# Strassen weight differences in slots on another grid, and one product of 512 columns at the head of each Strassen tile

## The chip, the cores and the metric

The kernel runs on one core of one Trainium2 chip. The engines are TensorE (PE in the profile; its weight loads are PEld), VectorE (DVE), ScalarE (ACT), GpSimd (POOL) and SyncE (SP, which issues the DMAs). The metric is the device time of one execution in microseconds, as the median of several runs.

## What is computed

A trunk of two layers on x with 256 rows and a width of 2048, all in float32. Layer 0 is a recurrent block, layer 1 attention over a sliding window; each is followed by a SwiGLU FFN with 5632 hidden columns. The change touches the first half of the FFN:

```python
def swiglu_ffn(x, g, w_in, w_out):
    h = rms_norm(x, g)
    gate, up = jnp.split(h @ w_in, 2, axis=-1)
    return x + (jax.nn.silu(gate) * up) @ w_out
```

## The kernel before

**Products.** TensorE multiplies in a float32 format that keeps fewer bits, so every operand is split into a high part and a low part (`hi`, `lo`), and one product becomes three: high by high, high by low, low by high. A weight tile of 128 x 1024 arrives by DMA in `raw`; ScalarE copies it to `hi` (L306, L299) and VectorE subtracts to get `lo` (L309, L300). `raw`, `hi` and `lo` are rings of four tiles. The x tiles and everything else live in 58 slots of 128 x 512 (`s0` to `s57`), handed out by `slot` and given back by `free`; x keeps its high part in the first 256 columns of a slot and its low part in the others.

An ordinary job works one weight tile off: 48 products of 256 columns with weights from hi/lo and the moving operand from a slot (L375; in the profile `b<-s,hi` means output, moving operand, weights). A product can also be 512 columns wide: it takes the high and the low part of x in one go and writes two halves of a PSUM bank. `products` makes them in runs of three (`RUNS`) where a bank has both halves free; the jobs between Strassen tiles share banks and have none.

**Strassen tiles.** In each FFN the first four column groups (`NS`) are done with seven multiplications of half blocks in place of eight (Strassen's scheme in Winograd's form). Each group has eight tiles, `c` from 0 to 7, so an FFN has 32. A tile is 7 x 3 = 21 products of 256 columns (L476) into four banks, here with weights from slots (x tiles, and sums of x tiles made by `form`) and the moving operand from hi/lo (`b<-hi,s`) or from slots that hold differences of weight blocks (`b<-s,s`). Between two Strassen tiles stand two ordinary jobs (`OWN`). The differences: GpSimd makes them from `raw` (`sums`, L279 to L281), ScalarE copies the high parts (L289), VectorE subtracts for the low parts (L291). `split_sums` issues this two jobs ahead of the tile, behind the split of a weight tile on the same engines. Two sets of six slots alternate: s[0] and s[1] hold the differences, s[2] to s[5] the parts; before, s[4] holds the high and s[5] the low part of s[1], so a high part and its low part are in different slots. In the tiles 1 to 6 of a group the nine products with hi/lo come first, in the tiles 0 and 7 six of them come ahead of the first with a difference.

Behind the last tile of a group `fast` (L675 to L685) adds the four banks up to the outputs U and V on VectorE (L132); a task then does the gate with two activations and two operations of L136, transposes the result on TensorE (L386) and splits it.

**The planner.** Queues are filled in program order, but the tool that lowers the kernel may place an instruction later than it is written. Background tasks are run by `run_bg` twice a job: a credit per engine (`dve`, `act`) rises by the estimated time of all that is issued and falls by one tick each half job, not below -SPARE; a task's next step runs only while `dve` is below DVE_TICK and `act` below ACT_TICK. In FFN 1 tick and floor are 640 and 500 for VectorE; from the K/V projection on 740 and 1000 (`LATER`). An add of n columns books 69 + 1.042 n.

**Where tiles stand.** Tiles take addresses in the order of their first use. Behind the lo ring come `t`, `h`, two `rstd` tiles of 258 columns, and further tiles of 256 columns, then the slots.

Of the kernel before, what the change touches and what calls it, by code (L numbers as in the profile page):

```python
# [12 lines left out]
F32 = mybir.dt.float32  # L13
F32R = mybir.dt.float32r
AF = mybir.ActivationFunctionType
ALU = mybir.AluOpType

P = 128
# [31 lines left out]
class Trunk:  # L50
# [24 lines left out]
    def __init__(self, ctx, tc, dram):  # L75
        self.tc, self.nc, self.d = tc, tc.nc, dram
        nc = self.nc
        const = ctx.enter_context(tc.tile_pool(name="const", bufs=1))
        psum = ctx.enter_context(tc.tile_pool(name="psum", bufs=1, space=bass.MemoryType.PSUM))
        tmp = ctx.enter_context(tc.tile_pool(name="tmp", bufs=1))  # L80
        self.tmp = tmp
        self.par = const.tile([P, NPAR], F32, name="par")
        self.con = const.tile([P, NCON], F32, name="con")
        self.cc = const.tile([P, 32], F32, name="cc")
        self.x = [const.tile([P, 4, T], F32, name=f"x{i}") for i in range(4)]
        self.slots = deque(range(58))
        self.spool = const
        self.held = {}
        self.raw = [const.tile([P, 1024], F32, name=f"raw{i}") for i in range(4)]
        self.hi = [const.tile([P, 1024], F32R, name=f"hi{i}") for i in range(4)]  # L90
        self.lo = [const.tile([P, 1024], F32R, name=f"lo{i}") for i in range(4)]
        self.banks = deque(psum.tile([P, 512], F32, name=f"b{i}") for i in range(8))
        self.misc = 0
        self.started = False
        self.xin = 0
        self.other = None
        self.summing = False
        self.opening = None
        self.sets = None
        self.runs = 0  # L100
        self.since = 0
        self.hold = False
        self.tmps = deque(const.tile([P, T], F32, name=f"t{i}") for i in range(4))
        self.halves = deque(const.tile([P, T], F32, name=f"h{i}") for i in range(8))
        self.rstd = [const.tile([P, T + 2], F32, name=f"rstd{i}") for i in range(2)]
        self.acc = const.tile([P, T], F32, name="acc")
        self.sq = deque(const.tile([P, T], F32, name=f"sq{i}") for i in range(2))
        self.jobs = []
        self.bg = deque()
        self.tick = -2 * self.LD  # L110
        self.dve = 0.0
        self.act = 0.0
# [34 lines left out]
        self.nc.vector.reciprocal(out, a)  # L147


    def slot(self, dt=F32R):  # L150
        i = self.slots.popleft()
        s = self.spool.tile([P, 2 * T], dt, tag=f"s{i}", name=f"s{i}")
        self.held[id(s)] = (i, s)
        return s

    def free(self, s):
        self.slots.append(self.held.pop(id(s))[0])

    def half(self):
        if self.halves:  # L160
            return self.halves.popleft()
        s = self.slot(F32)
        h = s[:, 0:T]
        self.held[id(h)] = (s, h)
        return h
# [103 lines left out]
    def sums(self, i):  # L269

        raw, tt = self.raw[i % 4], self.nc.gpsimd.tensor_tensor
        if not self.sets:
            self.sets = deque([self.slot(F32), self.slot(F32)] + [self.slot() for _ in range(4)] for _ in range(2))
        s = self.sets.popleft()
        self.sets.append(s)
        self.jobs[i][2]["set"] = s
        b = raw[:, :].rearrange("p (b t) -> p b t", b=4)
        two = lambda q: q.rearrange("p (b t) -> p b t", b=2)
        tt(two(s[0][:, :]), b[:, 0:3:2, :], b[:, 1::-1, :], ALU.subtract)  # L279
        tt(s[1][:, 0:T], raw[:, 2 * T:3 * T], s[0][:, 0:T], ALU.subtract)  # L280
        tt(s[1][:, T:2 * T], raw[:, 3 * T:4 * T], s[1][:, 0:T], ALU.subtract)  # L281

    def split_sums(self, i):

        if len(self.jobs[i]) > 2:
            s = self.jobs[i][2]["set"]
            for z, a, b in ((s[0], s[2], s[3]), (s[1], s[4], s[5])):
                with self.tc.issue_after(self.behind[0]):
                    self.nc.scalar.activation(a, z, AF.Copy)  # L289
                with self.tc.issue_after(self.behind[1]):  # L290
                    self.nc.vector.tensor_tensor(b, z, a.bitcast(F32), ALU.subtract)  # L291
            self.dve += 1400
            self.act += 1200
# [152 lines left out]
    def strassen(self, src, xs, forms, done, last, left):  # L446

        st = {}
        jobs = []
        for c in range(ND // 2):  # L450
            part = {}

            def mm(hi, lo, c=c, part=part):
                if c == 0:
                    st["ps"] = [self.bank() for _ in range(4)]
                    st["begun"] = set()
                ps = st["ps"]
                x2 = [self.need(xs[2 * c + kt]) for kt in range(2)]
                fh, fl = self.need(forms[c])
                A = lambda kt, b: tuple(x2[kt][:, q + b * P:q + b * P + P] for q in (0, T))  # L460
                S = lambda n: tuple(q[:, n * P:n * P + P] for q in (fh, fl))
                B = lambda n: tuple(q[:, n * T:n * T + T] for q in (hi, lo))
                s = part["set"]
                t1, t3, t2, t4 = (tuple(s[n + q][:, h * T:h * T + T] for q in (0, 1)) for n in (2, 4) for h in range(2))
                todo = [(0, 0, A(0, 0), B(1)), (1, 1, A(1, 0), B(3)), (1, 0, S(1), t2), (2, 0, S(0), t1),
                        (2, 1, S(2), t3), (3, 0, S(3), B(2)), (3, 1, A(1, 1), t4)]
                if 0 < c < ND // 2 - 1:
                    todo = [todo[q] for q in (0, 1, 5, 3, 4, 2, 6)]
                if self.other is not None:
                    self.runs = self.RUNS  # L470
                    self.other = None
                for n, (b, h, w, m) in enumerate(todo):
                    if n == 4:
                        self.half_tick()
                    for i, j in ((0, 0), (0, 1), (1, 0)):
                        self.nc.tensor.matmul(ps[b][:, h * T:h * T + T], w[i], m[j], start=b not in st["begun"],  # L476
                                              stop=c == ND // 2 - 1 and i == 1, skip_group_check=True)
                        st["begun"].add(b)
                        self.since += 1
                left[0] -= 1  # L480
                if last and c == ND // 2 - 1:
                    for q in self.sets:
                        for t in q:
                            self.free(t)
                    self.sets = None
                if last:
                    for q in (fh, fl):
                        self.free(q)
                if c == ND // 2 - 1:
                    done(ps)  # L490
            jobs.append((src(c), mm, part))
        return jobs

# [63 lines left out]

    def prep_tile(self, k, gains):

        self.gained(k, gains)  # L560
        yield
        yield from self.squares(k)
# [91 lines left out]
    def ffn(self, l, xs, forms, r, gains, rn, out=None):  # L654
# [6 lines left out]
        def later(g, s):  # L661
            while left[0]:
                yield 1
            for h in range(2):
                while len(self.slots) < 2:
                    yield 1
                q = self.slot()
                self.split_act(q, s[:, h * T:h * T + T])
                hid[2 * g + h].ap = q
                hid[2 * g + h].ready = True  # L670
                yield
            self.free(s)

        for g in range(self.NS):
            def fast(ps, g=g):  # L675
                c1, U, V = self.t(), self.slot(F32), self.slot(F32)
                two = lambda q: q.rearrange("p (b t) -> p b t", b=2)
                twice = lambda q: q.unsqueeze(1).broadcast_to([P, 2, T])
                self.a(c1, ps[0][:, 0:T])
                self.tt(two(U[:, :]), two(ps[1][:, :]), twice(c1[:, :]), ALU.add)  # L680
                self.tt(two(V[:, :]), two(ps[2][:, :]), twice(U[:, 0:T]), ALU.add)
                self.tt(U[:, 0:T], ps[2][:, 0:T], V[:, T:2 * T], ALU.add)
                self.tt(V, ps[3], V, ALU.add)
                for b in ps:
                    self.free_bank(b)  # L685

                def task():
# [26 lines left out]
        for g in range(self.NS, NH // 2):  # L714
            def done(ps, g=g):
# [4 lines left out]
                def task():  # L720
# [3 lines left out]
                    for h in range(2):  # L724
# [3 lines left out]
                            self.tt(up, up, rs, ALU.mult)  # L728
                        self.a(ga, ga, AF.Silu)
                        yield  # L730
                        if both is not None or h == 0 and left[0]:
                            if h == 0:
                                both = self.slot(F32)
                            self.tt(both[:, h * T:h * T + T], ga, up, ALU.mult)
# [638 lines left out]
```

## Time and profile before

| | us |
|---|---|
| median of three runs (lowest, highest) | 1974.23 (1973.96, 1975.21) |
| the profiled execution | 1976.51 |
| its span, first to last instruction | 1974.7 |
| L476, products of Strassen tiles, 1344 | 8% of the chain |
| L375, ordinary products | 84% of the chain |

How to read it: the profile's chain is followed back from the last instruction to what released it each time, so its shares say which engine's work the time consists of. TensorE's matmuls overlap, and an engine that is "busy" the whole span can still work at a slower or a faster pace; the pace is the distance from one product's start to the next. A group's row has its count, the busy time of the group, the mean duration of one in ns, and the idle time of the engine ahead of them.

### The profile page before, as it was taken

The numbers are of one execution on the slowest core, as the hardware profiler recorded it, in microseconds if no ns is written. First come the engines' busy times: TensorE is split into PE (matmuls) and PEld (weight loads), VectorE is DVE, ScalarE is ACT, GpSimd is POOL, SyncE is SP. The second block draws the span as 40 slices with busy tenths as digits, with TensorE's granted clock in tenths as the row PEclk, the third lists the DMA queues.
The fourth block names the chain that finished last, engine by engine and source line by source line (L and its number), as shares of the span: only waits on it lengthen the run. The fifth ranks groups of instructions, "written<-read, shape, count | busy, mean of one in ns | idle before, by whom it ended". The sixth has DMA issues, their size and how long they took to land.

```text
span 1974.7 us, 40978 instructions
## 1 busy us (share of the span) xinstructions
PE 1966.7 (100%) x16762; PEld 1934.6 (98%) x16762; DVE 1428.8 (72%) x2073; ACT 1121.2 (57%) x1746; POOL 383.4 (19%) x356
## 2 busy tenths in 40 slices
PE   9999999999999999999999999999999999999999
PEld 9999999999999999999999889999999999999999
DVE  8988978988986655545668767888889665554443
ACT  6798766555555444434556776655556554444442
POOL 0000125555520000000002454354444000000000
PEclk9999999999999999999999999999999999999999
DMA  8555665665555555555555434565555656556664
GB/s 276 187 190 177 200 209 193 187 208 197 192 201 191 195 193 192 193 193 196 195 185 182 129 129 152 191 214 193 193 193 201 194 193 193 194 196 205 206 205 127
DMA packets 106204, 377.16 MB, mean 191 GB/s; under 512 B 11936, under 2 KB 14368, under 8 KB 106016
## 3 DMA queue, kind: packets, MB, share of 16 engines
q1 hardware_dynamic: 105408, 373.88, 57.7%
q8 instruction: 131, 2.15, 0.4%
q10 hardware_dynamic: 608, 0.66, 0.1%
q14 instruction: 57, 0.47, 0.1%
HBM read 371.88 MB, written 2.10 MB: 189 GB/s over the span
## 4 chain that ended last, share of the span: by engine, by line
PE 96%; DVE 2%; ACT 1%; issue 0%; POOL 0%; DMA 0%; ACTq 0%; DVEq 0%; POOLq 0%
PE b L375 84%; PE b L476 8%; PE b L386 1%; PE b L866 1%; PE b L383 1%; ACT s L123 1%; DVE lo L309 1%; PE b L1052 1%; ACT hi L306 0%; DVE s L1120 0%; DVE s L132 0%; DMA x<-in_x 0%; PE b L1061 0%; PE b L1062 0%; PE b L1063 0%
## 5 line engine op out<-in xcount | busy, mean ns | idle before, releaser
L375 PE MATMUL b<-s,hi 128*128 128x256 f32 (+1 forms) x9536 | 1301.0, 282 | 1.6 <-ACT s L123 1.0
L375 PEld LDWEIGHTS b<-s,hi 128*128 128x128 f32 x9536 | 1203.1, 188 | 21.4 <-ACT s L123 1.7
L309 DVE TENSOR_TENSOR lo<-raw,hi 128x1024 fp32r<-128x1024 f32 (+1 forms) x643 | 812.5, 1266 | 447.4 <-ACT hi L306 444.8
L306 ACT ACTIVATE hi<-raw 128x1024 fp32r<-128x1024 f32 (+1 forms) x643 | 676.0, 1054 | 588.6 <-PE b L375 508.1
L375 PE MATMUL b<-s,lo 128*128 128x256 f32 x4992 | 748.3, 277 | 0.0
L375 PEld LDWEIGHTS b<-s,lo 128*128 128x128 f32 x4992 | 651.0, 188 | 0.5
L279 POOL TENSOR_TENSOR s<-raw 128x512 f32<-128x512 f32 x64 | 120.8, 1888 | 233.3 <-DMA raw<-in_ffn_in 185.6
L291 DVE TENSOR_TENSOR s<-s,s 128x512 fp32r<-128x512 f32 x128 | 141.5, 1141 | 0.6 <-ACT s L289 0.3
L1142 POOL TENSOR_TENSOR s<-s 128x128 f32<-128x128 f32 x32 | 14.7, 462 | 537.0 <-ACT s L123 534.3
L476 PE MATMUL b<-s,s 128*128 128x256 f32 x768 | 105.6, 282 | 0.5 <-DVE s L291 0.5
L299 ACT ACTIVATE hi<-raw 128x768 fp32r<-128x768 f32 x64 | 54.1, 845 | 78.8 <-PE b L375 56.5
L476 PEld LDWEIGHTS b<-s,s 128*128 128x128 f32 x768 | 97.3, 189 | 0.8 <-DVE s L291 0.7
L123 ACT ACTIVATE s<-s 128x256 fp32r<-128x256 f32 (+3 forms) x180 | 69.1, 429 | 33.4 <-POOL s L508 19.5
L132 DVE TENSOR_TENSOR s<-s,s 128x256 fp32r<-128x256 f32 (+3 forms) x148 | 70.6, 509 | 19.8 <-ACT s L123 19.7
L476 PE MATMUL b<-hi,s 128*128 128x256 f32 x384 | 80.7, 281 | 0.0
L280 POOL TENSOR_TENSOR s<-raw,s 128x256 f32<-128x256 f32 x64 | 78.7, 1230 | 5.0
L300 DVE TENSOR_TENSOR lo<-raw,hi 128x768 fp32r<-128x768 f32 x64 | 70.5, 1102 | 12.6 <-PE b L375 8.1
L289 ACT ACTIVATE s<-s 128x512 fp32r<-128x512 f32 x128 | 73.6, 617 | 7.8 <-POOL s L281 7.8
L506 POOL TENSOR_TENSOR s<-s 128x128 f32<-128x128 f32 x16 | 14.0, 877 | 328.8 <-ACT s L123 328.8
L281 POOL TENSOR_TENSOR s<-raw,s 128x256 f32<-128x256 f32 x64 | 70.9, 1108 | 5.0
L476 PEld LDWEIGHTS b<-hi,s 128*128 128x128 f32 x384 | 64.6, 189 | 0.0
L123 ACT ACTIVATE s<-x,par 128x256 fp32r<-128x256 f32 (+1 forms) x112 | 52.6, 498 | 19.9 <-DVE x L132 13.5
(121 smaller groups left out, 1127.4 us busy)
## 6 DMA issues: line engine op xcount, KB each, us to landing
raw<-in_ffn_in SPq DMA_DIRECT2D x352, 512.0 KB, 3.5
raw<-in_ffn_out SPq DMA_DIRECT2D x176, 512.0 KB, 3.4
raw<-in_lru_in SPq DMA_DIRECT2D x62, 512.0 KB, 3.6
raw<-in_lru_out SPq DMA_DIRECT2D x32, 512.0 KB, 3.8
raw<-in_w_q SPq DMA_DIRECT2D x32, 512.0 KB, 3.4
raw<-in_w_o SPq DMA_DIRECT2D x32, 512.0 KB, 3.3
raw<-in_gate SPq DMA_DIRECT2D x8, 512.0 KB, 3.7
raw<-in_kv SPq DMA_DIRECT2D x8, 512.0 KB, 3.4
```

The source lines that it names most:

```text
L123: self.nc.scalar.activation(out, in_, func, **kw)
L132: self.nc.vector.tensor_tensor(out, a, b, op)
L279: tt(two(s[0][:, :]), b[:, 0:3:2, :], b[:, 1::-1, :], ALU.subtract)
L280: tt(s[1][:, 0:T], raw[:, 2 * T:3 * T], s[0][:, 0:T], ALU.subtract)
L281: tt(s[1][:, T:2 * T], raw[:, 3 * T:4 * T], s[1][:, 0:T], ALU.subtract)
L289: self.nc.scalar.activation(a, z, AF.Copy)
L291: self.nc.vector.tensor_tensor(b, z, a.bitcast(F32), ALU.subtract)
L300: low = self.nc.vector.tensor_tensor(lo[:, q], raw[:, q], hi[:, q].bitcast(F32), ALU.subtract)
L306: high = self.ins(self.nc.scalar.activation(hi[:, q], raw[:, q], AF.Copy))
L309: low = self.nc.vector.tensor_tensor(lo[:, q], raw[:, q], hi[:, q].bitcast(F32), ALU.subtract)
L375: self.nc.tensor.matmul(*args, **kw)
L476: self.nc.tensor.matmul(ps[b][:, h * T:h * T + T], w[i], m[j], start=b not in st["begun"], stop=c == ND // 2 - 1 and i == 1, skip_group_ch ...
```

## The change

The 58 slots become 50 ordinary ones and eight others (`odd`, slots 50 to 57), which are claimed right behind the lo ring. The four split slots of both difference sets are taken from these; outside the FFN's Strassen phase, float32 slots are taken from them where one is free. Conditions on free slots now count the 50 alone. s[1] is split in two halves: s[4] holds the high and low part of its first half, s[5] those of its second. So s[5] can be read by one product of 512 columns. Each tile begins with it: A(1,1) high by both parts of t4, into both halves of bank 0, followed by A(1,1) low by t4 high. A(0,0) by B(1) goes to bank 3 in its place, and `fast` is rewritten for it: one more copy on ScalarE, and three adds of 256 columns in place of one of 512. The order of the seven multiplications is new.

```diff
-        self.slots = deque(range(58))
+        self.slots = deque(range(50))
+        self.odd = deque(range(50, 58))
...
+        for i in self.odd:
+            self.spool.tile([P, 2 * T], F32R, tag=f"s{i}", name=f"s{i}")
...
-    def slot(self, dt=F32R):
-        i = self.slots.popleft()
+    def slot(self, dt=F32R, odd=None):
+        odd = bool(self.odd) and dt == F32 if odd is None else odd
+        i = (self.odd if odd else self.slots).popleft()
...
-            self.sets = deque([self.slot(F32), self.slot(F32)] + [self.slot() for _ in range(4)] for _ in range(2))
+            self.sets = deque([self.slot(F32, False) for _ in range(2)] + [self.slot(F32R, True) for _ in range(4)]
+                              for _ in range(2))
...
-            for z, a, b in ((s[0], s[2], s[3]), (s[1], s[4], s[5])):
+            for z, a, b in ((s[0], s[2], s[3]), (s[1][:, 0:T], s[4][:, 0:T], s[4][:, T:2 * T]),
+                            (s[1][:, T:2 * T], s[5][:, 0:T], s[5][:, T:2 * T])):
...
-                todo = [(0, 0, A(0, 0), B(1)), (1, 1, A(1, 0), B(3)), (1, 0, S(1), t2), (2, 0, S(0), t1),
-                        (2, 1, S(2), t3), (3, 0, S(3), B(2)), (3, 1, A(1, 1), t4)]
+                todo = [(0, 0, A(1, 1), t4), (3, 1, A(0, 0), B(1)), (1, 0, S(1), t2), (1, 1, A(1, 0), B(3)),
+                        (2, 0, S(0), t1), (2, 1, S(2), t3), (3, 0, S(3), B(2))]
                 if 0 < c < ND // 2 - 1:
-                    todo = [todo[q] for q in (0, 1, 5, 3, 4, 2, 6)]
+                    todo = [todo[q] for q in (0, 1, 3, 6, 4, 5, 2)]
...
-                    for i, j in ((0, 0), (0, 1), (1, 0)):
+                    if n == 0:
+                        self.nc.tensor.matmul(ps[b], w[0], s[5], start=b not in st["begun"],
+                                              stop=c == ND // 2 - 1, skip_group_check=True)
+                        st["begun"].add(b)
+                    for i, j in ((0, 0), (0, 1), (1, 0))[2 * (n == 0):]:
...
     def prep_tile(self, k, gains):
+        while len(self.slots) < 3:
+            yield 1
...
-                while len(self.slots) < 2:
+                while len(self.slots) < 4:
...
-                c1, U, V = self.t(), self.slot(F32), self.slot(F32)
+                c1, c4, U, V = self.t(), self.t(), self.slot(F32), self.slot(F32)
...
-                self.a(c1, ps[0][:, 0:T])
+                self.a(c1, ps[3][:, T:2 * T])
                 self.tt(two(U[:, :]), two(ps[1][:, :]), twice(c1[:, :]), ALU.add)
                 self.tt(two(V[:, :]), two(ps[2][:, :]), twice(U[:, 0:T]), ALU.add)
+                self.a(c4, ps[0][:, T:2 * T])
                 self.tt(U[:, 0:T], ps[2][:, 0:T], V[:, T:2 * T], ALU.add)
-                self.tt(V, ps[3], V, ALU.add)
-                for b in ps:
+                self.tt(V[:, 0:T], ps[3][:, 0:T], V[:, 0:T], ALU.add)
+                self.tt(V[:, T:2 * T], ps[0][:, 0:T], V[:, T:2 * T], ALU.add)
+                self.tt(V[:, T:2 * T], V[:, T:2 * T], c4, ALU.add)
+                for b in (ps[1], ps[2], ps[3], ps[0]):
                     self.free_bank(b)
...
-                        if both is not None or h == 0 and left[0]:
+                        if both is not None or h == 0 and (left[0] or len(self.slots) < 8):
+                            while h == 0 and not (self.slots or self.odd):
+                                yield 1
```

More of the change, by code (lines that the diff above doesn't have):

```diff
@@ L156, in free @@
     def free(self, s):
-        self.slots.append(self.held.pop(id(s))[0])
+        i = self.held.pop(id(s))[0]
+        (self.slots if i < 50 else self.odd).append(i)
     def half(self):
@@ L161, in half @@
             return self.halves.popleft()
-        s = self.slot(F32)
+        s = self.slot(F32, False)
         h = s[:, 0:T]
@@ L463, in mm @@
                 s = part["set"]
-                t1, t3, t2, t4 = (tuple(s[n + q][:, h * T:h * T + T] for q in (0, 1)) for n in (2, 4) for h in range(2))
-                todo = [(0, 0, A(0, 0), B(1)), (1, 1, A(1, 0), B(3)), (1, 0, S(1), t2), (2, 0, S(0), t1),
-                        (2, 1, S(2), t3), (3, 0, S(3), B(2)), (3, 1, A(1, 1), t4)]
+                t1, t3 = (tuple(s[2 + q][:, h * T:h * T + T] for q in (0, 1)) for h in range(2))
+                t2, t4 = (tuple(q[:, h * T:h * T + T] for h in range(2)) for q in s[4:6])
+                todo = [(0, 0, A(1, 1), t4), (3, 1, A(0, 0), B(1)), (1, 0, S(1), t2), (1, 1, A(1, 0), B(3)),
+                        (2, 0, S(0), t1), (2, 1, S(2), t3), (3, 0, S(3), B(2))]
                 if 0 < c < ND // 2 - 1:
-                    todo = [todo[q] for q in (0, 1, 5, 3, 4, 2, 6)]
+                    todo = [todo[q] for q in (0, 1, 3, 6, 4, 5, 2)]
                 if self.other is not None:
```

## The prediction

> **What bounds the kernel now.** First the profile page: its busy line and its chain by line.
>
> ```profile
> span 1974.7 us, 40978 instructions
> ...
> PE 1966.7 (100%) x16762; PEld 1934.6 (98%) x16762; DVE 1428.8 (72%) x2073; ACT 1121.2 (57%) x1746; POOL 383.4 (19%) x356
> ...
> PE b L375 84%; PE b L476 8%; PE b L386 1%; PE b L866 1%; PE b L383 1%; ACT s L123 1%; DVE lo L309 1%; PE b L1052 1%; ACT hi L306 0%; DVE s L1120 0%; DVE s L132 0%; DMA x<-in_x 0%; PE b L1061 0%; PE b L1062 0%; PE b L1063 0%
> ```
>
> TensorE is the chain. It hardly ever waits, so the time is the number of products times the pace at which they follow each other. Second, the chain in order of time inside the first FFN (start, length, line, products), at the end of one Strassen group and the begin of the next:
>
> ```profile
> 359.51 5.44 PE b L375 x48
> 364.96 2.49 PE b L476 x21
> ...
> 372.89 2.48 PE b L476 x21
> 375.38 5.65 PE b L375 x48
> 381.03 2.46 PE b L476 x21
> 383.49 4.24 PE b L375 x36
> ```
>
> Products of the same width run at two paces: 5.44/48 = 0.1133 us, or 5.65/48 = 0.1177 us. A Strassen tile in mid-group takes 2.49/21 = 0.1186 us per product, and the ordinary work returns to 0.1133 behind it; behind a group's last tile (375.38) and behind its first (383.49) it stays slow. Third, what decides the pace: the K/V projection, where twelve ordinary products (weights from hi/lo, moving operand from a slot, L1052) alternate with twelve whose operands are swapped (L1061 to L1063, as in a Strassen tile).
>
> ```profile
> 1009.91 1.36 PE b L1052 x12
> 1011.28 0.12 PE b L1061
> ...
> 1012.69 1.41 PE b L1052 x12
> 1014.11 0.12 PE b L1061
> ...
> 1015.48 1.36 PE b L1052 x12
> ```
>
> From start to start: ordinary 1.37, swapped 1.41, ordinary 1.42, swapped 1.37, ordinary 1.36. So the pace is a state that is handed on: ordinary fast makes swapped slow, swapped slow makes ordinary slow, ordinary slow makes swapped fast, and swapped fast gives ordinary fast back. Both kinds can run at 0.1133.
>
> **The change, part by part.** *Placement.* In a Strassen tile all weights come from slots; of its 21 products nine have their moving operand in hi/lo and twelve in difference slots. Two `rstd` tiles of 258 columns stand between the lo tiles and the slots, 2 x 8 bytes off the grid of all other tiles; slots 50 to 57, now claimed right behind lo, stand on the grid of hi/lo. So all products of a tile become "swapped" in the sense of the K/V rows, where twelve now read slot against slot. *The 512-column product* at the head must turn the state that ordinary-fast hands over into swapped-fast. Its length, from a timeline in which three of them and two products of 256 columns fill one group:
>
> ```profile
> 208.27 1.08 PE L375 MATMUL b<-s,hi 128*128 128x512 f32 x5
> 209.19 0.62 PE L375 MATMUL b<-s,lo 128*128 128x256 f32 x4
> ```
>
> (209.19 - 208.27 - 2 x 0.1133)/3 = 0.231 us. No row shows one such product alone at the head of swapped work. The code sets them in runs of three elsewhere; that one alone shifts the state the right way is the unknown. Bounds: no tile reaches the fast pace, or all do.
>
> Fast tile: 19 x 0.1133 + 0.231 = 2.384 us. 48 tiles in mid-group save 2.49 - 2.384 = 0.106, the first two of each of 8 groups 2.46 - 2.384 = 0.076: 5.1 + 1.2 = **6.3 us**. Ordinary stretches behind last tiles: 8 x (5.65 - 5.44) = **1.7 us**. Behind first tiles transposes enter the stream, and half of 8 x 0.21 is taken: **0.8 us**. Gain 8.8, at most 9.7.
>
> *The wait.* The 512-column product reads s[5], which the last VectorE operation of L291 writes. Before, six or nine products on hi/lo stood ahead of the first use of these slots. In mid-group that costs nothing: two L291 end at 360.36 + 2.39 = 362.75, the tile begins at 364.96.
>
> ```profile
> 360.36 2.39 DVE L291 TENSOR_TENSOR s<-s,s 128x512 fp32r<-128x512 f32 x2
> ```
>
> At the group boundary it isn't so. The table by stage (length, then busy us of TensorE, its weight loads, VectorE, ScalarE, GpSimd), and VectorE's timeline beside that of TensorE's first product:
>
> ```profile
> 1334.00:1351.00 17.00, 17.00 (x146) 17.00 (x145) 16.52 (x22) 10.42 (x17) 7.00 (x6) 1.00 0.57 180
> 1351.00:1398.00 47.00, 47.00 (x412) 47.00 (x411) 39.08 (x38) 24.25 (x33) 24.61 (x19) 1.00 0.63 205
> ```
> ```profile
> 374.86 1.95 DVE L132 TENSOR_TENSOR s<-b,s 128x512 f32<-128x512 f32 x3
> ...
> 378.77 2.37 DVE L291 TENSOR_TENSOR s<-s,s 128x512 fp32r<-128x512 f32 x2
> ...
> 382.20 0.87 DVE L136 SCALAR_TENSOR_TENSOR s<-s,rstd,s 128x256 f32<-128x256 f32 x2
> ```
> ```profile
> 380.87 0.28 PE L476 MATMUL b<-hi,s 128*128 128x256 f32 x1
> ```
> ```profile
> 1339.93 1.83 DVE L136 SCALAR_TENSOR_TENSOR s<-s,rstd,s 128x256 f32<-128x256 f32 x2
> 1341.69 1.28 DVE L291 TENSOR_TENSOR s<-s,s 128x512 fp32r<-128x512 f32 x2
> ```
> ```profile
> 1342.27 0.28 PE L476 MATMUL b<-hi,s 128*128 128x256 f32 x1
> ```
>
> VectorE is at 16.52 of 17 us there, against 39.08 of 47 behind. The split ends 381.14 - 380.87 = 0.27 us behind the first tile's begin in FFN 1, and 1342.97 - 1342.27 = 0.70 in FFN 2. Now hidden, later a stall. `fast` grows too: one 512-column add becomes three of 256.
>
> ```profile
> L132 DVE TENSOR_TENSOR s<-b,s 128x512 f32<-128x512 f32 x16 | 11.1, 692 | 1.7
> L132 DVE TENSOR_TENSOR s<-b,s 128x256 f32<-128x256 f32 x8 | 3.4, 424 | 0.3
> L132 DVE TENSOR_TENSOR s<-s,s 128x256 fp32r<-128x256 f32 x96 | 42.2, 479 | 0.9 <-ACT s L123 0.9
> ```
>
> 3 x 0.424 - 0.692 = 0.58 us more on VectorE ahead of the split, with L309 and L291 queued behind it and TensorE behind these. The split of s[1] in two halves: 2 x 0.479 = 0.96 against 0.64 to 1.20 for one of 512 (the two L291 rows above, halved): between -0.24 and +0.32, taken as 0. And TensorE arrives 0.11 + 0.21 = 0.31 earlier, which gives back its own gain.
>
> Later groups of FFN 1: 0.1 (between 0 and 0.27) + 0.58 + 0.31 = 1.0 each, **3.0**. Later groups of FFN 2: 0.70 + 0.58 + 0.31 = 1.6, but the planner's credit moves something: from its floor of -1000, `fast` books 2143 now and 2548 after; less one tick of 740 that is 403 (under 740, so the L136 pair is issued ahead of the split, as the row at 1339.93 shows) against 808 (over it, so the pair falls behind the split, as in FFN 1 at 382.20). That takes 1341.69 - 1339.93 = 1.76 away from ahead of the first tile; the pair then delays the second by some 0.9, and I take 0.5 per group, **1.5**. If the credit isn't at the floor: 4.8. First groups:
>
> ```profile
> 316.49 1.22 DVE L291 TENSOR_TENSOR s<-s,s 128x512 fp32r<-128x512 f32 x1
> ...
> 323.10 2.94 DVE L291 TENSOR_TENSOR s<-s,s 128x512 fp32r<-128x512 f32 x2
> ...
> 1278.43 0.68 DVE L291 TENSOR_TENSOR s<-s,s 128x512 fp32r<-128x512 f32 x1
> ```
> ```profile
> 316.94 0.28 PE L476 MATMUL b<-hi,s 128*128 128x256 f32 x1
> ...
> 325.17 0.28 PE L476 MATMUL b<-hi,s 128*128 128x256 f32 x1
> ...
> 1277.70 0.28 PE L476 MATMUL b<-hi,s 128*128 128x256 f32 x1
> ...
> 1279.16 0.39 PE L476 MATMUL b<-s,s 128*128 128x256 f32 x1 [0.49 <-DVE s L291]
> ```
>
> FFN 1: 317.71 - 316.94 = 0.77 at the first tile, 326.04 - 325.17 = 0.87 at the second; VectorE does not pause between them, so what the first tile waits the second needn't, and together it is 0.9, with an earlier arrival 1.0. FFN 2: 1279.11 - 1277.70 = 1.41, of which about 0.65 is paid today (the stall at 1279.16), and a little at the second tile: 1.0. **2.0** in all. A few mid-group tiles that are as late: **0.5**. Waits 7.0, between 3.5 (only what is late today) and 11.
>
> *At nothing:* the extra ScalarE work (two short copies per tile for one long, one in `fast`), as ScalarE is busy 24.25 of 47 us. The planner's stricter counts of free slots hold back x splits in FFN 1's output projection until its last column group frees slots; there VectorE has 23 us to spare in 59, and without that cover it costs 1 to 2 us at the K/V projection.
>
> ```profile
> 950.00:1009.00 59.00, 59.00 (x514) 58.63 (x513) 36.21 (x48) 31.83 (x44) 0.00 (x0) 1.00 0.60 194
> ```
>
> **Sum.** -8.8 + 7.0 = -1.8 us. The profiled execution's span is 1974.7 (1976.51 with what lies around it, 2.3 above the median of the three timed runs); the difference goes onto the median: 1974.23 - 1.8 = **1972.4 us**.
>
> **A rule against the change.** The Trainium skill ("SBUF — State Buffer", section "Who interferes with whom") says that PE never waits on anyone and has independent ports for moving operand and weights; by it, placement buys nothing. The K/V rows contradict it as far as pace goes: identical products, no engine waited for, 1.36 against 1.41. That placement is the reason no row shows.
>
> **Rivals.** *Waits are mostly covered* (B). The queues aren't in written order: the L136 pair stands at two different places. If TensorE's queue puts products on hi/lo ahead of the 512-column one, or VectorE's puts L291 ahead of `fast`, 2 us of waits remain: 1974.2 - 8.8 + 2 = 1967.4. Against it: at 1279.16 TensorE stood still while products on hi/lo of the same tile were ready. *The wrong state* (C, slower). The 512-column product leaves a tile slow; slow swapped makes ordinary slow, and the next tile starts from there. Place: behind all 48 mid-group tiles; price 0.21 each, 10.1 us, with waits of about 4 (TensorE arrives later): 1988. It decides at the tile's second product: 0.118 instead of 0.113. *The change doesn't do what it says* (D): placement has nothing to do with pace; gain 0, and the waits without the earlier arrivals (7.0 less 6 x 0.31) are 5.1: 1979.3.
>
> **Chances.** Forecast (A), gain mostly given back: 0.45, its own range 1970.4 to 1978. B 0.30, C 0.13, D 0.12. A measurement of this kernel can tell about 0.2%, 3.9 us, from no change: B is faster (0.30), A the same (0.45), C and D slower (0.25). The range takes in B down to 1965.5 (9.7 gained, 1 lost) and D with waits at their upper end less the earlier arrivals (11 - 1.9, 1983.3): up to 1984. It leaves out most of C.
>
> **What would show it.** Right: in the chain, L476 stretches of 20 products in 2.38 to 2.39; ordinary stretches of 5.44 behind last tiles; TensorE waiting for L291 about 7 us in all, at the first two tiles of groups; the L136 pair behind L291 in both FFNs. Wrong: tiles at 2.48 with 5.65 behind them (C), tiles at 2.48 with 5.44 (D), or waits for L291 under 3 us (B).

## The result: slower, by waits far larger than forecast

| | before | after |
|---|---|---|
| median, us (lowest, highest) | 1974.55 (1973.96, 1975.21) | 1994.86 (1994.31, 1999.02) |
| span of the profiled execution, us | 1974.7 | 1993.3 |

The ratio is 1.0107, with a 95% interval of 1.009 to 1.0125. The forecast was 1972.4, with a range up to 1984: the kernel became 20 us slower where a gain of 2 was expected. One more run, the first of the edit called "Bank 3 early" below, had a granted clock of 0.616 and took 2975.94 us, so it says nothing of that edit, which was run again. In the kernel after, L484 is the product of 512 columns, L488 the other products of Strassen tiles, L382 the ordinary ones, L298 the VectorE part of `split_sums`, L126 ScalarE's helper and L135 VectorE's. The "head" of a tile is its product of 512 columns; t1 and t3 are the two halves of the first difference s[0], t2 and t4 those of the second, s[1].

First the page after: busy shares and the chain by line.

```profile
PE 1967.3 (99%) x16698; PEld 1928.9 (97%) x16698; DVE 1438.7 (72%) x2153; ACT 1128.0 (57%) x1818; POOL 371.8 (19%) x356
...
PE b L382 78%; PE b L488 7%; ACT s L126 2%; DVE lo L316 1%; ACT hi L313 1%; DVE s L298 1%; PE b L484 1%; PE b L393 1%; DVE s L135 1%; ACT L126 1%; PE b L1071 1%; DVE s L1139 1%; PE b L390 0%; POOL s L1205 0%; POOL s L1163 0%
```

TensorE is busy 1967.3 us against 1966.7 before, in a span that is 18.6 us longer: it has not more to do, it stands still for longer. Its share of the chain has gone to ScalarE, VectorE and GpSimd. Next the chain in order of time, over the same boundary between two groups that the prediction showed (start, length, line, products).

```profile
341.72 0.23 PE b L484
341.95 2.15 PE b L488 x19
344.10 5.44 PE b L382 x48
...
378.04 1.88 DVE lo L316
...
382.94 0.50 PE b L484
...
385.45 5.65 PE b L382 x48
```

In mid-group a tile takes 0.23 + 2.15 = 2.38 us, as forecast, and hands over to 5.44. At the boundary the chain leaves TensorE for VectorE, and behind the stall the ordinary stretch is slow (5.65). Third, what TensorE waited for (us in total, times, longest), before and after:

```profile
PE b L476 <- DVE s L291: 0.5, 1, 0.5
PE b L383 <- POOL s L1186: 0.3, 1, 0.3
```
```profile
PE b L484 <- DVE s L298: 15.6, 16, 1.7
PE b L390 <- POOL s L1205: 4.4, 3, 2.5
```

Both waits have grown from next to nothing. How much they weigh shows in a sum over the products of the weight tiles and of the attention (transposes and the start of the kernel aside). What is added up is the time from one start to the next, beyond 0.1133 us for 256 columns. I call it slow pace where it is 1.5 to 16 ns per product and a stall where it is more:

| us | before | after |
|---|---|---|
| slow pace, Strassen products | 6.6 | 2.2 |
| slow pace, ordinary products | 10.2 | 10.9 |
| stalls at and in Strassen tiles | 1.4 | 21.2 |
| stalls in ordinary work and the attention | 10.6 | 13.6 |

That is +19.1 us, half a microsecond more than the spans differ (18.6).

Why the head waits is seen at that boundary. First ScalarE and VectorE of before, then these two and TensorE of after (start, length, engine, line, what; in brackets the idle time before and what ended it):

```profile
373.28 0.38 ACT L123 ACTIVATE t<-b 128x256 f32<-128x256 f32 x1 [0.41 <-PE b L476]
...
374.06 0.69 DVE L132 TENSOR_TENSOR s<-b,t 128x512 f32<-128x512 f32 x1
```
```profile
376.22 0.39 ACT L126 ACTIVATE t<-b 128x256 f32<-128x256 f32 x1 [1.66 <-PE b L488]
...
376.63 0.69 DVE L135 TENSOR_TENSOR s<-b,t 128x512 f32<-128x512 f32 x1 [1.75 <-ACT t L126]
...
382.14 0.75 DVE L298 TENSOR_TENSOR s<-s,s 128x256 fp32r<-128x256 f32 x2
...
381.58 0.28 PE L488 MATMUL b<-lo,s 128*128 128x256 f32 x1
382.94 0.50 PE L484 MATMUL b<-s,s 128*128 128x512 f32 x1 [1.08 <-DVE s L298]
```

Before, `fast` copied c1 from bank 0, which the tile finishes early; the copy stood 0.39 us behind the tile's begin (372.89), and VectorE went on without a pause. After, c1 comes from the second half of bank 3. That half is finished by the second of the seven multiplications, but the last one writes the other half of the same bank, and the copy starts only behind it: it is at 376.22, 2.4 us behind the tile's begin (373.78), VectorE idles 1.75 us, and the adds, the split queued behind them and TensorE are late by as much. The stall is 382.94 - 381.58 - 0.11 = 1.25 us.

A second place was not foreseen: tiles in mid-group. Here the sixth tile of the second group, before and after:

```profile
417.53 2.93 DVE L291 TENSOR_TENSOR s<-s,s 128x512 fp32r<-128x512 f32 x2
...
421.12 0.28 PE L476 MATMUL b<-hi,s 128*128 128x256 f32 x1
```
```profile
419.81 3.55 DVE L298 TENSOR_TENSOR s<-s,s 128x512 fp32r<-128x512 f32 x3
...
423.41 0.50 PE L484 MATMUL b<-s,s 128*128 128x512 f32 x1 [0.45 <-DVE s L298]
```

Before, two operations took 2.93 us and ended 0.66 us ahead of the tile (421.12). Three take 3.55 us, and the tile waits 0.61 us for the last. That is 1.27 us to the worse: 0.62 us for the longer split, and the rest because TensorE comes sooner behind the split's begin. Taken from TensorE's starts as in the 1.25 above, the eight first tiles of groups lose 11.7 us (1.1 to 1.9 each) and eight later tiles, all of them third or sixth tiles, 6.6 (0.6 to 1.3 each).

### The profile page after: what moved, and what is told of

The parts are those of the page before. It is cut to its first block, busy times and chain, and to the rows that moved or that the text cites. A ratio compares the mean times of both kernels' runs of the same rounds, so it can differ in the third digit from the quotient of the medians.

```text
span 1993.3 us, 41074 instructions
## 1 busy us (share of the span) xinstructions
PE 1967.3 (99%) x16698; PEld 1928.9 (97%) x16698; DVE 1438.7 (72%) x2153; ACT 1128.0 (57%) x1818; POOL 371.8 (19%) x356
## 4 chain that ended last, share of the span: by engine, by line
PE 89%; DVE 5%; ACT 4%; issue 1%; POOL 1%; DMA 0%; ACTq 0%; DVEq 0%; POOLq 0%
PE b L382 78%; PE b L488 7%; ACT s L126 2%; DVE lo L316 1%; ACT hi L313 1%; DVE s L298 1%; PE b L484 1%; PE b L393 1%; DVE s L135 1%; ACT L126 1%; PE b L1071 1%; DVE s L1139 1%; PE b L390 0%; POOL s L1205 0%; POOL s L1163 0%
## 5 line engine op out<-in xcount | busy, mean ns | idle before, releaser
L382 PE MATMUL b<-s,hi 128*128 128x256 f32 (+1 forms) x9536 | 1300.6, 282 | 1.2 <-DVE h L135 0.6
L382 PEld LDWEIGHTS b<-s,hi 128*128 128x128 f32 x9536 | 1203.2, 188 | 21.0 <-ACT s L126 1.3
L316 DVE TENSOR_TENSOR lo<-raw,hi 128x1024 fp32r<-128x1024 f32 (+1 forms) x643 | 804.3, 1253 | 444.9 <-ACT hi L313 442.0
L382 PE MATMUL b<-s,lo 128*128 128x256 f32 x4992 | 748.2, 277 | 0.0
L382 PEld LDWEIGHTS b<-s,lo 128*128 128x128 f32 x4992 | 651.1, 188 | 0.5
L298 DVE TENSOR_TENSOR s<-s,s 128x256 fp32r<-128x256 f32 (+1 forms) x192 | 156.4, 863 | 0.0
L126 ACT ACTIVATE s<-s 128x256 fp32r<-128x256 f32 (+3 forms) x208 | 80.3, 426 | 41.5 <-POOL s L520 19.5
L135 DVE TENSOR_TENSOR s<-s,s 128x256 fp32r<-128x256 f32 (+3 forms) x176 | 85.2, 514 | 22.8 <-ACT s L126 22.4
L488 PE MATMUL b<-s,s 128*128 128x256 f32 x640 | 96.8, 278 | 0.0
L488 PEld LDWEIGHTS b<-s,s 128*128 128x128 f32 x640 | 84.0, 188 | 0.0
L488 PE MATMUL b<-hi,s 128*128 128x256 f32 x384 | 82.1, 278 | 0.0
L296 ACT ACTIVATE s<-s 128x256 fp32r<-128x256 f32 (+1 forms) x192 | 79.0, 473 | 2.3 <-POOL s L287 2.3
L286 POOL TENSOR_TENSOR s<-raw,s 128x256 f32<-128x256 f32 x64 | 73.6, 1150 | 5.0
L488 PEld LDWEIGHTS b<-hi,s 128*128 128x128 f32 x384 | 65.2, 188 | 2.8
L287 POOL TENSOR_TENSOR s<-raw,s 128x256 f32<-128x256 f32 x64 | 63.6, 994 | 5.0
L126 ACT ACTIVATE s<-x,par 128x256 fp32r<-128x256 f32 (+1 forms) x112 | 52.5, 498 | 20.2 <-DVE x L135 12.4
```

Source lines behind the costliest of these rows:

```text
L126: self.nc.scalar.activation(out, in_, func, **kw)
L135: self.nc.vector.tensor_tensor(out, a, b, op)
L316: low = self.nc.vector.tensor_tensor(lo[:, q], raw[:, q], hi[:, q].bitcast(F32), ALU.subtract)
L382: self.nc.tensor.matmul(*args, **kw)
```

## Experiments: the pace

Three of these four kernels were run once, beside one run of before. Runs of one kernel differ by up to 3 us, so these totals can't settle small differences; the rows on pace can.

**Head of two products of 256 columns** (placement kept).

```diff
-    self.nc.tensor.matmul(ps[b], w[0], s[5], start=b not in st["begun"], ...)
+    for q in range(2):
+        self.nc.tensor.matmul(ps[b][:, q * T:q * T + T], w[0], s[5][:, q * T:q * T + T], ...)
```

> The changed kernel with its one 512-column product per tile replaced by two products of 256 columns (same sums). Theory W (the pace is won by placement and the 512-column head together; the loss is waits): without the head a tile entered from fast ordinary work stays slow, so mid-group tiles take 21 x 0.118 = 2.47 to 2.49 us instead of 2.385, and the ordinary stretch behind them is slow too (5.65); the total rises by up to 48 x (0.10 + 0.21) = 15 us, less what the later arrival saves in waits (some 5): 2000 to 2008. Rival P (placement alone makes the pace): tiles stay at 2.38 and the total at 1994 to 1996.

Measured 1993.19 us (one run; before in the same set 1975.91).

```profile
348.08 2.15 PE b L490 x19
...
355.91 2.24 PE b L490 x19
358.15 5.65 PE b L382 x48
...
PE b L485 <- DVE s L298: 11.1, 11, 1.6
```

The tiles alternate between 2.39 and 2.48 (2.15 and 2.24 behind the two products of the head), so the slow pace costs 3.2 us in Strassen products and 13.4 in ordinary ones, 3.5 more than in the change, while the waits fall by 4.5. In the change, where stalls cut it short, the 512 columns are thus worth 3.5 us of pace; without them the kernel is slower, waits less, and ends at about the same time. Both expected ranges were above the result.

**Odd slots on the grid of the others** (head kept): the eight are claimed behind `sq`, not behind lo.

```diff
-        for i in self.odd:
-            self.spool.tile([P, 2 * T], F32R, tag=f"s{i}", name=f"s{i}")
...
         self.sq = deque(const.tile([P, T], F32, name=f"sq{i}") for i in range(2))
+        for i in self.odd:
+            self.spool.tile([P, 2 * T], F32R, tag=f"s{i}", name=f"s{i}")
```

> The changed kernel with the eight difference slots claimed behind the rstd tiles, so that they stand on the grid of the other slots, the 512-column head kept. Theory W: twelve products of a tile read slot against slot again, at 0.118 to 0.120: mid-group tiles 2.45 to 2.50 us, total 1997 to 2005. Rival H (the head alone makes the pace): tiles stay at 2.385 and the total at 1994 to 1996.

Measured 1996.0 us (one run), with 12.3 us of waits at heads. A mid-group tile took 2.45 us in the stretch below (342.20 to 344.65):

```profile
342.20 0.23 PE b L484
342.44 2.21 PE b L488 x19
```

Without the placement no tile of the 64 is faster than 2.45: that placement has to do with pace, which was an inference, is shown. That the offset of 16 bytes is what counts, and not something else about the place, is not shown.

**The slots alone**: order of products, split and `fast` as before the change (cut; three of the places that go back).

```diff
-            for z, a, b in ((s[0], s[2], s[3]), (s[1][:, 0:T], s[4][:, 0:T], s[4][:, T:2 * T]),
-                            (s[1][:, T:2 * T], s[5][:, 0:T], s[5][:, T:2 * T])):
+            for z, a, b in ((s[0], s[2], s[3]), (s[1], s[4], s[5])):
...
-                    if n == 0:
-                        self.nc.tensor.matmul(ps[b], w[0], s[5], start=b not in st["begun"],
...
-                self.a(c1, ps[3][:, T:2 * T])
+                self.a(c1, ps[0][:, 0:T])
```

> Only the first part of the change: 50 slots and 8 odd ones, placed as in the change, with its counts of free slots; the order of products, the two split operations and `fast` are those of before. Theory S (the smaller pool of slots is what costs some 3 us in the attention between the two feed-forward parts, as waits of TensorE for GpSimd): 1977 to 1979 us with 3 to 4.5 us of such waits. Rival (those waits come from where the first feed-forward part ends, by its timing): 1974 to 1976 us, with under 1 us of them. By either, no waits of over 1 us at the heads of Strassen tiles.

Measured 1978.68 us (ratio 1.0022, 1.0012 to 1.0031).

```profile
341.23 2.48 PE b L482 x21
343.71 5.65 PE b L381 x48
349.36 2.39 PE b L482 x21
351.76 5.44 PE b L381 x48
...
PE b L389 <- POOL s L1196: 1.9, 2, 1.6
```

Placement alone makes every second tile fast and the ordinary work between slow and fast in turn: 2.48 + 5.65 + 2.39 + 5.44 = 15.96 us for two tiles with the work behind them, against 2 x (2.49 + 5.44) = 15.86 before. So placement and the head of 512 columns pay only together. The slots also bring a wait for GpSimd in the attention, 1.9 us of it here, where TensorE's and GpSimd's instructions come in the same order as before and only VectorE's and ScalarE's differ (0.3 us before, 4.4 in the change). The total lies in the range expected of the slots, the wait below it.

**The head reads what is ready**: its 512 columns are two blocks of hi, and the third product moves to the tile's end. This kernel leaves out the sums with t4 but for that third product, so it doesn't compute the FFN; it shows times alone.

```diff
-    self.nc.tensor.matmul(ps[b], w[0], s[5], start=b not in st["begun"], ...)
+    self.nc.tensor.matmul(ps[b], w[0], hi[:, T:3 * T], start=b not in st["begun"], ...)
...
-                    for i, j in ((0, 0), (0, 1), (1, 0))[2 * (n == 0):]:
+                    for i, j in ((0, 0), (0, 1), (1, 0))[3 * (n == 0):]:
...
+                b, h, w, m = todo[0]
+                self.nc.tensor.matmul(ps[b][:, h * T:h * T + T], w[1], m[0], start=False,
...
```

> The changed kernel in which the 512-column head reads two weight blocks of hi in place of the last difference, and the product of the low part of A(1,1) with the high part of t4 stands at the end of the tile: the sums with t4 are left out but for the last one, no tile waits for a difference at its head. Theory W (18 us of waits at the heads): most of the 18 us go, what is left is at the first product on a difference, about 1 us later: total 1977 to 1983. Rival Q (VectorE as a whole is short, and the waits move to wherever its results are needed next): total 1988 to 1995.

Measured 1974.69 us (one run; 1975.91 before).

```profile
PE b L488 <- DVE s L298: 2.8, 7, 0.7
```

The waits at the head are gone; what is left is at the first product on a difference. Slow pace costs 0.6 us in Strassen and 7.4 in ordinary products, 6.6 + 10.2 - 0.6 - 7.4 = 8.8 us less than before: the size of the gain that was forecast. The total came out below the range expected, which was worked out from the waits alone; the pace of ordinary work is better too (7.4 against 10.9 in the change).

## Experiments: the waits

Three things make t4 late: `fast` starts late (bank 3), there are three operations in place of two, and t4 is the last of them. Each is taken away by itself and with others. "The same set" below means the runs of before that were made together with the run in question.

**Bank 3 early**: the last tile of a group takes its products in another order.

```diff
                 if 0 < c < ND // 2 - 1:
                     todo = [todo[q] for q in (0, 1, 3, 6, 4, 5, 2)]
+                elif c:
+                    todo = [todo[q] for q in (0, 1, 6, 2, 3, 4, 5)]
```

> The last tile of each group now runs its products in the order that finishes bank 3 third, so that the copy c1 no longer waits for the tile's end. Theory G (the gate: the last unsplit difference is late at the first tile of a group because the end work of the group before, `fast`, starts 1.7 to 2.5 us later than it did): the six waits at first tiles of later groups, 8.5 us together, fall under 1.5, and with the pace behind them the time comes to 1985 to 1988 us. Theory O (three split operations where there were two are what is late, whatever stands before them): these waits fall by under 2 us, 1992 to 1995 us.

Measured 1989.17 us (ratio 1.0077, 1.006 to 1.0094).

```profile
373.09 0.38 ACT L126 ACTIVATE t<-b 128x256 f32<-128x256 f32 x1 [0.30 <-PE b L490]
...
PE b L486 <- DVE s L298: 11.5, 15, 1.6
```

The copy c1 now stands 1.1 us behind the tile's begin (372.02) in place of 2.4. The effect on the waits is right in its direction and too small: the six first tiles of later groups fell from 8.5 to 5.2 us, not under 1.5. t4, the third operation, is still 0.6 us late in four of these places and 1.2 to 1.5 us in two, and the time is above theory G's range.

**Two operations again**: the halves of s[1] lie side by side in one tile of 1024 columns. The eight odd slots become four and two such tiles, in the same room; so outside the FFN there are six places for float32 slots in place of eight.

```diff
-            for z, a, b in ((s[0], s[2], s[3]), (s[1][:, 0:T], s[4][:, 0:T], s[4][:, T:2 * T]),
-                            (s[1][:, T:2 * T], s[5][:, 0:T], s[5][:, T:2 * T])):
+            two = lambda q: q.rearrange("p (b t) -> p b t", b=2)
+            wide = s[4][:, :].rearrange("p (b q t) -> p b q t", b=2, q=2)
+            for z, a, b in ((s[0], s[2], s[3]), (two(s[1][:, :]), wide[:, :, 0, :], wide[:, :, 1, :])):
...
```

> The two halves of the second difference are split again by one operation on each engine, as before the change: the two slots of each set that hold them lie side by side in one tile of 1024 columns. The order of products and `fast` stay those of the change. Theory O: the waits at the third and sixth tiles (some 6 us) go, and each first tile of a group waits some 0.5 us less; waits at heads 18 to under 10 us, 1983 to 1987 us. Theory G: the first tiles keep their 8.5 us, since the copy from bank 3 starts all of it; over 1987 us.

Measured 1983.91 us (ratio 1.005, 1.0035 to 1.0065).

```profile
PE b L489 <- DVE s L303: 10.4, 11, 1.3
```

The time is that of theory O. The first tiles of later groups still lose 1.24 to 1.41 each, which is what theory G said of them; later tiles lose some 2 us in place of 6.6.

**t4 first**, the smallest edit: the three operations in another order.

```diff
-            for z, a, b in ((s[0], s[2], s[3]), (s[1][:, 0:T], s[4][:, 0:T], s[4][:, T:2 * T]),
-                            (s[1][:, T:2 * T], s[5][:, 0:T], s[5][:, T:2 * T])):
+            for z, a, b in ((s[1][:, T:2 * T], s[5][:, 0:T], s[5][:, T:2 * T]), (s[0], s[2], s[3]),
+                            (s[1][:, 0:T], s[4][:, 0:T], s[4][:, T:2 * T])):
```

> The change with one thing swapped: of its three split operations the half that the head reads (t4) comes first; three operations and the late bank 3 stay. Theory Z (the head's place at the end of the queue of splits is most of the cost): the waits at the heads of third and sixth tiles go, those of first tiles, 8.5 us, lose the two operations ahead of them (0.9 us alone to 2.4 us beside GpSimd, six times) and fall under 3; 1975 to 1980 us. Theory G (the late bank 3 decides at first tiles, whatever the order): they stay above 5 us, over 1982 us.

Measured 1980.27 us (ratio 1.0026, 1.0017 to 1.0036), 0.3 us above the range of theory Z and 1.7 under that of theory G.

```profile
PE b L488 <- DVE s L298: 3.3, 8, 0.7
PE b L484 <- DVE s L298: 2.1, 4, 0.9
```

This order alone gives 14.4 of the 20.3 us back. Of the waits that are left, 3.3 us are at the third multiplication of first tiles, which now waits for the last operation (t2), and 2.1 us at heads. The waits of third tiles have gone; two sixth tiles still lose 1.1 and 0.9 us.

**Bank 3 early and t4 first**, three operations kept (the two edits above together):

> Three split operations as in the change, bank 3 early, and the half that the head reads (t4) split first of the three. By theory Z the head then waits for the first operation instead of the third one, and most of the 11.5 us of waits left with bank 3 early alone go from the heads, but t2, now third, is late for the third product of first and last tiles; 1974 to 1980 us. By theory O three operations are too long in whatever order, since GpSimd makes each cost over 1 us: over 1984 us.

Measured 1973.86 us (ratio 0.9994, 0.9985 to 1.0004): just below the 1974 to 1980 of theory Z, and far from theory O.

```profile
PE b L486 <- DVE s L298: 1.8, 4, 0.7
PE b L490 <- DVE s L298: 1.3, 3, 0.7
```

**Bank 3 early and two operations**, again two edits from above (the text calls the kernel below, with 1972.1 us, the run before this one):

> The run before this one with the first difference split ahead of the second, as in the change: so two split operations and the early bank 3 alone. From the change these two took off 10.9 and 5.7 us one at a time, 16.6 us together, which leads from 1994.9 to 1978.3 us; both with the swapped order of the splits came to 1972.1. Theory N (the swap does nothing, the two parts help each other since each wait they shorten is cut at zero by the other): 1971 to 1974 us. Theory Z (the swap is worth the missing 6 us): 1976 to 1979 us, with waits of 0.3 to 0.8 us at the heads of several tiles.

Measured 1979.22 us (ratio 1.0019, 1.0009 to 1.0028); 0.2 us above the range of theory Z, and over 5 us above that of theory N.

```profile
379.01 1.23 DVE L303 TENSOR_TENSOR s<-s,s 128x512 fp32r<-128x512 f32 x1
...
PE b L491 <- DVE s L303: 6.3, 11, 1.4
```

Each first tile of a later group still loses 0.56 or 0.57 us. The split of t4 stands behind that of the other difference and behind the last add of `fast`, and ends at 380.24; in the kernel below it ends at 377.85 for the same tile.

**All three** (two operations, bank 3 early, and the second difference ahead of the first in the loop):

> Both edits at once, and the second difference is split ahead of the first one, since the first product of a tile reads it. If gate and operations together are the whole of the waits at heads, these fall under 2 us, the faster products of the change (8.8 us) stay, and the attention keeps its 3 us: 1968 to 1973 us, faster than before the change. If a third cause is left (a late GpSimd difference, a queue), over 1978 us.

Measured 1972.12 us (ratio 0.9987, 0.9978 to 0.9997): in the range expected.

```profile
374.10 5.44 PE b L387 x48
379.54 0.23 PE b L491
379.77 2.15 PE b L495 x19
381.92 5.45 PE b L387 x48
...
377.05 0.80 DVE L303 TENSOR_TENSOR s<-s,s 128x512 fp32r<-128x512 f32 x1
...
379.37 0.39 PE L491 MATMUL b<-s,s 128*128 128x512 f32 x1
...
PE b L491 <- DVE s L303: 0.7, 2, 0.4
```

The chain runs over the boundary (379.54) on TensorE alone, at the fast pace on both sides; the split that the head reads ends at 377.85, 1.5 us ahead of it. Waits at heads are down to 0.7 us; those for GpSimd in the attention are 2.8 us, as was expected.

**Free slots counted as before**: the all-three kernel with one count set back.

```diff
-                while len(self.slots) < 4:
+                while len(self.slots) < 2:
```

> The 1972.1 us kernel (two operations, bank 3 early, second difference first), with the count of free slots that the hidden vectors' split waits for back at 2 in place of 4: only the order of work at the end of each feed-forward part changes. Theory H (this count costs nothing, as predicted): within 1 us of 1972.1. Rival (it costs 1 to 2 us): 1970 to 1971 us.

Measured 1971.8 us (ratio 0.9983, 0.9973 to 0.9992): within 1 us of 1972.1, as theory H has it. But less before in the same set it is -3.4 us where the kernel above is -2.0, and the intervals overlap: the run can't tell a count that costs nothing from one that costs the rival's 1 to 2 us. With the one above it is the fastest version found.

The table puts these kernels together as the median less that of before in the same set; by the intervals above each is uncertain by 2 to 3 us.

| us against before | bank 3 late | bank 3 early |
|---|---|---|
| three operations, t4 last | +20.3 (the change) | +15.0 |
| two operations, t4 in the last | +9.8 | +4.0 |
| three operations, t4 first | +5.9 | -1.4 |
| two operations, t4 in the first | not run | -2.0 |

With t4 first and bank 3 early, the number of operations is worth 0.6 us, which is within the noise; with t4 last, 10 to 11. So the third operation costs mainly since the head stood behind it. Where VectorE starts is worth 5 to 7 us in each row that has both.

## Why the prediction was wrong

**Pace: right.** The mid-group tile of 2.384 us, the ordinary stretch of 5.44 behind it and the gain of 8.8 us came as worked out once the waits were taken away (the head on ready data, in one run): 6.0 us in Strassen products where 6.3 were forecast, 2.8 in ordinary ones where 2.5 were. In the change itself a stall puts the next stretch back to 5.65, so it keeps only 6.6 + 10.2 - 2.2 - 10.9 = 3.7 us of it. That 512-column head and placement are both needed is shown; why the pace depends on them is not.

**The wait: the step that failed.** It was sized 7.0 us, with 11 as its upper end; the heads lost about 18. Term by term, forecast and measured: later groups of FFN 1 3.0 and 4.5, later groups of FFN 2 1.5 and 4.1, first groups 2.0 and 2.5 (3.2 less what was paid before), mid-group tiles 0.5 and 6.6. Four things were missing or too small in it:

- *The start of `fast`* was left where it was. The diff moves c1 to bank 3 while the order of the last tile closes that bank last; the extra operations of `fast` were priced (0.58 us) and its start not. Setting only this right is worth 5.3 us (bank 3 early against the change).
- *Mid-group tiles* were said to cost nothing, from one tile with 2.2 us to spare, and 0.5 us was kept for others. They cost 6.6. The trace of before had it: at the sixth tiles of groups the split ended only 0.66 us ahead of the tile in three groups, and at its begin or behind it in two.
- *The split of s[1] in two halves* was taken as 0, with 0.32 us as the upper bound. By the rows by form, one above the other,

```profile
L298 DVE TENSOR_TENSOR s<-s,s 128x256 fp32r<-128x256 f32 x128 | 90.8, 747 | 0.0
...
L298 DVE TENSOR_TENSOR s<-s,s 128x512 fp32r<-128x512 f32 x64 | 70.0, 1094 | 0.0
```

  two halves take 2 x 0.747 = 1.49 us and one whole 1.09, so they cost 0.40 in the mean, beyond the bound, and more where GpSimd works. The 0.479 came from operations of L132, not of the split. The Trainium skill ("SBUF — State Buffer", section "Who interferes with whom") says that a VectorE operation with two SBUF inputs contends with a GpSimd operation that reads SBUF; this trace agrees, with 0.41 us for a half alone and 0.95 as the median of those that GpSimd works beside for more than half of their time.
- *The order of the splits* was read rightly ("s[5], which the last VectorE operation of L291 writes") and not weighed: of the 20.3 us, 14.4 go when t4 comes first.

The L136 pair (L139 after) does fall behind the split in both FFNs, as forecast from the planner's credit (in FFN 2 below, the same boundary as in the prediction), and second tiles behind it did not wait. The 1.76 us that this was to take away from the first tiles did not help: they lost 1.1 to 1.6 us each. There too VectorE stood idle for 1.75 us ahead of `fast` (at 1349.70).

```profile
1354.84 1.28 DVE L298 TENSOR_TENSOR s<-s,s 128x256 fp32r<-128x256 f32 x2
1356.04 0.87 DVE L139 SCALAR_TENSOR_TENSOR s<-s,rstd,s 128x256 f32<-128x256 f32 x2
```

**At nothing: wrong by 2 us or more.** ScalarE's two short copies for one long cost no more than the noise, as said: with t4 first and bank 3 early, three operations with these copies are 0.6 us from two without. Whether the count of free slots in the hidden vectors' split costs anything stays open. But the slots alone make the kernel 4.5 us slower, of which 1.6 us are added waits for GpSimd in the attention; in the change these grew by 4.1. Its last one, and GpSimd's operations at the same place before:

```profile
1191.98 2.42 POOL L1186 TENSOR_TENSOR s<-s,con 128x256 f32<-128x256 f32 x2
```
```profile
1201.73 2.89 DVE L316 TENSOR_TENSOR lo<-raw,hi 128x1024 fp32r<-128x1024 f32 x2
1201.74 3.46 POOL L1205 TENSOR_TENSOR s<-s,con 128x256 f32<-128x256 f32 x2
...
1205.26 0.43 PE L390 MATMUL b<-s,s 128*64 128x256 f32 x1 [2.51 <-POOL s L1205]
```

After, two VectorE splits run back to back beside the two GpSimd operations, which take 3.46 us where they took 2.42. That is 1.0 of the 2.51 us; for the rest, TensorE comes to need them 1.0 us behind their begin where it was 2.6 before. Which of the reordered VectorE and ScalarE steps brings the splits there was not tried and stays open.

**The rivals.** The wrong state after the head (C) did not come: tiles take 2.38 us. That placement is irrelevant (D) fell with the run on the other grid. TensorE's queue did pull two ready products ahead of the head (381.58 above), a piece of B, but they cover only 0.23 us, and the stall behind them is 1.25. The slower end was on the list only through pace; the waits, its real cause, had no rival of their own above 11 us.

## What to carry to other kernels

When a product is moved to the head of a tile, the operand that it reads becomes the one with the earliest due time: follow it back through its whole queue, and move its producer to the front with it. For each read in rewritten end work, ask when its source is finished (here the whole bank, not the half that is read), not only what the read costs. A pace that depends on operands is real, but it is the first thing that a stall gives away again.

## What the runs showed of the hardware

- TensorE's pace for the same products depends on where the operands lie and on what ran just before. The 21 products of a tile took 2.49 us before, and 2.39 and 2.48 in turn with the slots alone; with both parts of the change, where two of them are one of 512 columns, they took 2.38. The sentence of the Trainium skill that the prediction weighed ("SBUF — State Buffer", section "Who interferes with whom"), that PE never waits on anyone, is about waits for other engines, and no run here tests that; the prediction's reading of it, that placement buys nothing, is what these rows contradict.
- An operation of VectorE on two SBUF operands costs only a quarter less for being half as large when GpSimd works beside it: 0.95 us for 256 columns (89 of them) and 1.24 for 512 (39), against 0.41 and 0.69 with GpSimd idle. These are medians over the split operations of the change, "beside" meaning more than half of their time.
